# The last product's weights are multiplied with the gate on GpSimd before their split, and what its banks held is added to the sum first

## The chip, the cores and the metric

The kernel runs on one core of one Trainium2 chip. The metric is the device time of one execution in microseconds, the median of several runs. The engines of the core are TensorE (PE, with its weight loads PEld), VectorE (DVE), ScalarE (ACT), GpSimd (POOL) and SyncE (SP), which issues most transfers.

## The reference, cut to what matters

One layer (`DEPTH = 1`) on 512 tokens of width 2048, and a last RMSNorm:

```python
mod = cond @ w_ada[l] + b_ada[l]
shift, scale, gate = jnp.split(mod, 3, axis=-1)
h = rms_norm(x, norm_g[l]) * (1.0 + scale[:, None, :]) + shift[:, None, :]
z = h @ w_in[l]
...
y = jnp.concatenate([y_a, y_b], axis=-1) @ w_out[l]
x = x + gate[:, None, :] * y
...
return rms_norm(x, final_g)
```

y_a comes from a spatial gating unit, y_b from an attention with forget gates. The change lies in the last three lines only: the product with w_out, the gate, the sum with x and the final norm. The gate is one number for each column of the output, so it can be multiplied with the columns of w_out ahead of the product as well as with the result behind it.

## The kernel before, in words

All matrix products are made in three passes. An operand is split in a high and a low half of float32r by `split` (L65): ScalarE copies to `hi`, VectorE (or GpSimd) takes `lo = src - hi`. A product is then hi·hi + lo·hi + hi·lo; `mm_part` (L1056) issues these three matmuls of 128x512 into one PSUM bank.

The stages before the last compute h, the projections, the gating unit and the attention; the gate's columns are summed on GpSimd in the middle of the kernel (`gate_step`, L714). The result y lies transposed in sixteen blocks of 128 rows and 512 tokens.

**The output projection.** It has 512 tokens and 2048 output columns, and is made in two units, `unit(0)` and `unit(1)` (L1110), of 1024 columns each: group g1 and group g2 of 512 columns. Inside a unit it is a fast 2x2 block product with seven block products in place of eight, in Winograd's form. The blocks are the two halves of the tokens (tiles t = 0, 1 and 2, 3 of 128 tokens), the two halves of y and the two column groups. Sums of w_out's blocks were made earlier and lie in DRAM (`tsum`). The order in a unit is A11, S3, S2, S1, A22, A12, S4. Each of them is eight k-blocks times two token tiles, 48 matmuls, into two banks (V, Z or X).

**Weights.** A product goes through four steps (`product`, L1062). For each step a weight tile `raw` of 128x1024 is loaded on SP (`wget` L1026 from w_out, or `w_sum` L1117 from `tsum`), split by `wsplit` (L1033: low half on VectorE, L67), and multiplied. The tag `raw` has four buffers, and the x tile of `base` (L1075) takes one of the four. The weights are named after their products: p5 for S1, p4 for A22, p2 for A12, p3 for S4.

**The last unit.** In `unit(1)` group g2 = 3 of the token tiles 0 and 1 is finished last. Its sum has the parts u2 (from S2 and A11), S1 and S4:

- `base` (L1075) makes u2·gate + x ahead of A12;
- S1 lies in the two banks Z; `u3 = Z + u3` (L1155) has read it for the other token tiles, and S4 accumulates on top of it in the same banks (`mm_part(..., False, ...)`, L1206);
- `total` (L1208) multiplies the bank Z = S1 + S4 with the gate into `tmp` (helper `gated`, L1072) and adds u2 (L1211);
- `norm` (L1213) squares the sum on ScalarE (L1092), adds the mean square to that of the other groups (L1216) and takes the power -1/2 on GpSimd (L1217); `put` (L1222) scales the rows and stores them.

S4's weights are loaded after A12's in the program and split in halves of 512 columns on their own (`w3h`, `w3l`, L1181 to L1188), with a priority that moves loads and splits forward. Ahead of the last product in the program stand the pieces of the other groups: `piece` (L1094) is a sum with x (L1087), a square (L1092) and a multiplication with final_g (L1098); `scale_out` (L1100) takes a power on GpSimd, then scales and stores the token tiles 2 and 3.

**What sets the order.** A scheduler orders each engine's instructions ahead of the run: the ready instruction that comes first in the program, where loads and splits of weights count as 150 instructions earlier (`high_priority(offset=WPRI)`), as do the reads of finished banks (`evac`, EPRI). Buffers of a tag are given out in this order when one comes free. On the chip each engine then follows its list strictly. `issue_after` fixes an order on one engine.

The functions that the diff touches:

Of the kernel before, what the change touches and what calls it, by code (L numbers as in the profile page):

```python
# [9 lines left out]
F32R = mybir.dt.float32r  # L10
BF16 = mybir.dt.bfloat16
AF = mybir.ActivationFunctionType
ALU = mybir.AluOpType
AX = mybir.AxisListType

P = 128
S = 512
# [10 lines left out]
def trunk_kernel(  # L28
# [17 lines left out]
    nc = tc.nc  # L46
# [12 lines left out]
    def bank(tag, name):  # L59
        if tag == "x":  # L60
            tag = "bbbc"[turn[0] % 4]
            turn[0] += 1
        return ps.tile([P, 512], F32, tag=tag, name=name, bufs={"mm": 4, "b": 3, "c": 1}[tag])

    def split(hi, lo, src, eng=None):  # L65
        a = nc.scalar.activation(hi, src, AF.Copy)  # L66
        return a, (eng or nc.vector).tensor_tensor(lo, src, hi.bitcast(F32), ALU.subtract)  # L67
# [34 lines left out]
    newest_mm = [None]  # L102
# [15 lines left out]
    WPRI = 150  # L118
# [4 lines left out]
    def w_tile(segs, k0, nk, src=win_r, name="", pri=WPRI, loeng=None, after=None):  # L123
        n = sum(w for _, w in segs)
        es = ExitStack()
        for p in list(pins):
            p[0] -= 1
            if p[0] < 0:
                es.enter_context(tc.issue_after(p[1].ins))
                pins.remove(p)  # L130
        with es, tc.high_priority(offset=pri):
            raw = wp.tile([P, nk, n], F32, tag="raw", name=f"raw_{name}", bufs=4)
            o = 0
            for c0, w in segs:
                newest_w[0] = (load if pri == 0 else nc.sync.dma_start)(
                    raw[:, :, o : o + w], src[:, k0 : k0 + nk, c0 : c0 + w]
                )
                o += w
            hi = wp.tile([P, nk, n], F32R, tag="whi", name=f"whi_{name}")
            lo = wp.tile([P, nk, n], F32R, tag="wlo", name=f"wlo_{name}")  # L140
            nc.scalar.activation(hi, raw, AF.Copy)  # L141
            with ExitStack() as es:
                if after is not None:
                    es.enter_context(tc.issue_after(after.ins))
                (loeng or nc.vector).tensor_tensor(lo, raw, hi.bitcast(F32), ALU.subtract)  # L145
        return hi, lo

    def tick():
        if slots:
            for f in slots.pop(0):  # L150
                f()
        if fillers:
            fillers.pop(0)()
# [88 lines left out]
    gate = gp_.tile([P, 4, 512], F32, name="gate")  # L242
# [211 lines left out]
    for q, (k0, nk) in enumerate(CH):  # L454
# [10 lines left out]
        for si, sid in enumerate(order):  # L465
# [12 lines left out]
            for kk, n_k, gi in steps:  # L478
                    segs, bl = grp[gi]
                    hi, lo = w_tile(  # L480
                        segs, kk, n_k, name=f"st{q}_{sid}_{gi}_{kk}", pri=0,
                        loeng=nc.gpsimd if gi in POOLG and q + kk + si > 0 else None,
                        after=first_h[0] if q + kk + si == 0 else None,
                    )
# [31 lines left out]
    pb = ctx.enter_context(tc.tile_pool(name="pb", bufs=1))  # L516
# [506 lines left out]
    def wtile(name):  # L1023
        return wp.tile([P, 2, 512], F32, tag="raw", name=name, bufs=4)

    def wget(dst, half, g, i):  # L1026
        k = 8 * half + 2 * i
        nc.sync.dma_start(dst, wout_r[:, k : k + 2, g * 512 : (g + 1) * 512])
        return dst
# [3 lines left out]
    def wsplit(src, name):  # L1033
        nsplit[0] += 1
        if nsplit[0] % 3 == 0:
            hi = pb.tile([P, 2, 512], F32R, tag="pth", name=f"whi_{name}")
            lo = pb.tile([P, 2, 512], F32R, tag="ptl", name=f"wlo_{name}")
        else:
            hi = wp.tile([P, 2, 512], F32R, tag="whi", name=f"whi_{name}")
            lo = wp.tile([P, 2, 512], F32R, tag="wlo", name=f"wlo_{name}")  # L1040
        newest_hl[:] = split(hi, lo, src)
        return hi, lo

    def lhs(kind, i, tt):
        if kind == "S4":
            c = slice(tt * P, (tt + 1) * P)
            return s4[i][:, 0, c], s4[i][:, 1, c]
        h_, l_, k, off = {
            "A11": (yh, yl, 8 + i, 0), "S3": (yh, yl, 8 + i, H),
            "A12": (yh, yl, i, 0), "A22": (yh, yl, i, H),  # L1050
            "S1": (sh_, sl_, i, 0), "S2": (sh_, sl_, i, H),
        }[kind]
        c = slice(off + tt * P, off + (tt + 1) * P)
        return h_[k][:, c], l_[k][:, c]

    def mm_part(bank_, kind, i, tt, hi, lo, begin, end):  # L1056
        h_, l_ = lhs(kind, i, tt)
        nc.tensor.matmul(bank_, h_, hi, start=begin, stop=False, skip_group_check=True)
        nc.tensor.matmul(bank_, l_, hi, start=False, stop=False, skip_group_check=True)  # L1059
        newest_mm[0] = nc.tensor.matmul(bank_, h_, lo, start=False, stop=end, skip_group_check=True)  # L1060

    def product(banks, kind, weights, begin, steps=range(4)):  # L1062
        for i2 in steps:
            with tc.high_priority(offset=WPRI):
                hi, lo = weights(i2)
            for j in range(2):
                for tt in range(2):
                    i = 2 * i2 + j
                    mm_part(banks[tt], kind, i, tt, hi[:, j, :], lo[:, j, :], begin and i == 0, i == 7)
            tick()  # L1070

    def gated(rr, src, g):  # L1072
        nc.vector.tensor_tensor(rr, src, gate[:, g, :], ALU.mult)

    def base(rr, g):  # L1075

        xr = wtile("xr3")
        for t in range(2):
            nc.sync.dma_start(xr[:, t, :], x[0, t * P : (t + 1) * P, g * 512 : (g + 1) * 512])
        for t in range(2):  # L1080
            gated(rr[t], rr[t], g)
            nc.vector.tensor_tensor(rr[t], rr[t], xr[:, t, :], ALU.add)
# [27 lines left out]
    def unit(u):  # L1110
        g1, g2 = 2 * u, 2 * u + 1
        V = [bank("mm", f"woV{u}_{t}") for t in range(2)]

        def w_raw(half, g, name):
            return lambda i: wsplit(wget(wtile(f"{name}_{u}_{i}"), half, g, i), f"{name}_{u}_{i}")
# [8 lines left out]
        def tiles(n, tag, b=2):  # L1124
            pool = act if tag == "yb" else pb
            return [pool.tile([P, S], F32, name=f"{n}{u}_{t}", tag=tag, bufs=b) for t in range(2)]

        def evac(f):
            with tc.high_priority(offset=EPRI):
                for t in range(2):  # L1130
                    f(t)
# [8 lines left out]
        Z = [bank("mm" if u else "x", f"woZ{u}_{t}") for t in range(2)]  # L1140
# [5 lines left out]
        if u:  # L1146
            wide = [pb.tile([P, 2, 512], F32, name=f"wide{t}", tag="wsp", bufs=2) for t in range(2)]
            u2, u3 = [w[:, 0, :] for w in wide], [w[:, 1, :] for w in wide]
        else:
            u2, u3 = tiles("u2", "yb", 8), tiles("u3", "yb", 8)  # L1150
# [16 lines left out]
        both(lambda t: gated(c7[t], c7[t], g1))  # L1167
        both(lambda t: piece(c7[t], 2 + t, g1))
        if u:
            base(u2, g2)  # L1170
        product(V, "A12", w_raw(0, g1, "p2"), False)
        evac(lambda t: gated(c1[t], V[t], g1))
        both(lambda t: piece(c1[t], t, g1))
        if u == 0:
# [2 lines left out]
            both(lambda t: gated(u2[t], u2[t], g2))  # L1177
            both(lambda t: piece(u2[t], t, g2))
            return
        w3 = []  # L1180
        for i in range(4):  # L1181
            with tc.high_priority(offset=WPRI):
                a = wget(wtile(f"p3_{u}_{i}"), 0, g2, i)
                for j in range(2):
                    hi = pb.tile([P, S], F32R, tag="qstk", bufs=8, name=f"w3h{2 * i + j}")
                    lo = pb.tile([P, S], F32R, tag="kstk", bufs=8, name=f"w3l{2 * i + j}")
                    split(hi, lo, a[:, j, :])
                    w3.append((hi, lo))  # L1188
        before = newest_mm[0]
        for t in range(2):  # L1190
            tk = 2 + t
# [9 lines left out]
        def mm(t):  # L1201
            for i in range(8):
                with ExitStack() as es:
                    if i == 0:
                        es.enter_context(tc.issue_after(before.ins))
                    mm_part(Z[t], "S4", i, t, w3[i][0], w3[i][1], False, i == 7)  # L1206

        def total(t):  # L1208
            tmp = pb.tile([P, S], F32, name=f"tmp{t}", tag="sgB", bufs=4)
            gated(tmp, Z[t], g2)  # L1210
            return tmp, nc.vector.tensor_tensor(u2[t], tmp, u2[t], ALU.add)  # L1211

        def norm(t, tmp):  # L1213
            s0, s1 = sfin[:, t, 0:1], sfin[:, t, 1:2]
# [7 lines left out]
        def put(t, g, eng, q):  # L1222
# [6 lines left out]
            q.dma_start(out[0, t * P : (t + 1) * P, g * 512 : (g + 1) * 512], rr)  # L1229

        mm(0)
        norm(0, total(0)[0])
        put(0, 0, nc.scalar, nc.sync)
        put(0, 1, nc.scalar, nc.sync)
        mm(1)
        tmp, last = total(1)
        with tc.issue_after(last.ins):
            put(0, 2, nc.vector, nc.sync)
# [8 lines left out]
    for u in range(2):  # L1247
        unit(u)
# [26 lines left out]
```

## Time and profile before

| | us |
|---|---|
| runs, median of 3 | 898.06 (897.68 to 898.46) |
| the profiled execution | 899.12 |
| its span in the profile | 897.4 |
| granted TensorE clock | 0.997 |
| PE, DVE, ACT, POOL busy | 881.7, 614.7, 444.4, 479.7 |
| HBM read, written | 166.90 MB, 20.97 MB |

Lines such as `L1073` are lines of the kernel; helpers show their own line. A row of the timeline is start, duration, engine, line, operation, out<-in by tile name, shape, and in brackets how long the engine had been idle and what ended that. Buffer numbers are left out of tile names: `p` are the weight tiles p2 to p7 and p3, `wide` are u2 and u3 of unit 1, `c` are c1 and c7. Durations of neighbouring instructions on one engine overlap by some 0.08 us; the distance of their starts is what one costs in a full queue. In a table by stretches each engine has its busy time and, in brackets, its number of instructions; then come granted clock, DMA share and GB/s.

### The profile page before, as it was taken

How to read it: one execution, taken by the hardware profiler on the slowest of the kernel's cores; microseconds unless marked ns; L12 is line 12 of the kernel's file. 1: busy time of each engine (PE TensorE's matmuls, PEld its weight loads, DVE VectorE, ACT ScalarE, POOL GpSimd, SP SyncE). 2: the span in 40 equal slices, each digit the busy share in tenths (PEclk: the TensorE clock that was granted, in tenths of full speed). 3: DMA queues.
4: the chain of work that ended last, by engine and by line, in shares of the span. 5: the costliest groups of instructions: out<-in, count | busy, mean ns of one | idle time of the engine just before them, and what ended most of it. 6: DMA issues, size and time to landing. Idle time of an engine off the chain costs nothing.

```text
span 897.4 us, 12688 instructions
## 1 busy us (share of the span) xinstructions
PE 881.7 (98%) x4453; PEld 744.7 (83%) x4453; DVE 614.7 (68%) x999; ACT 444.4 (50%) x778; POOL 479.7 (53%) x407
## 2 busy tenths in 40 slices
PE   9999999999999999999999999999999999999995
PEld 6788888887888897887889888998898888888884
DVE  5878888374427967563876664547664779997686
ACT  6653333452224224564656554556466567654454
POOL 1266554515676269999799779957566520000001
PEclk9999999999999999999999999999999999999998
DMA  9999996348986275544443536466666466577575
GB/s 340 354 352 355 354 344 205 111 134 284 331 285 200 61 212 155 156 139 136 142 150 117 187 107 188 129 193 198 222 188 211 165 214 200 174 263 244 178 245 195
DMA packets 123216, 188.91 MB, mean 211 GB/s; under 512 B 9856, under 2 KB 86864, under 8 KB 122640
## 3 DMA queue, kind: packets, MB, share of 16 engines
q1 hardware_dynamic: 113248, 153.97, 53.6%
q0 software_dynamic: 9472, 33.56, 11.6%
q8 instruction: 35, 0.57, 0.3%
q10 hardware_dynamic: 432, 0.57, 0.2%
q14 instruction: 29, 0.24, 0.1%
HBM read 166.90 MB, written 20.97 MB: 209 GB/s over the span
## 4 chain that ended last, share of the span: by engine, by line
PE 89%; DMA 4%; DVE 3%; ACT 1%; issue 1%; SPq 1%; POOLq 0%; POOL 0%; ACTq 0%
PE s L163 6%; PE s L165 6%; PE s L164 6%; PE k L165 3%; PE gb L164 3%; PE gb L165 3%; PE gb L163 3%; PE k L164 3%; PE k L163 3%; PE vb L173 3%; PE vb L174 3%; PE va L175 3%; PE va L174 3%; PE va L173 3%; PE vb L175 3%; PE q L165 3%
## 5 line engine op out<-in xcount | busy, mean ns | idle before, releaser
L723 POOL TENSOR_SCALAR gate<-gate,sc 128x512 f32<-128x512 f32 x64 | 108.5, 1708 | 1.4
L727 POOL TENSOR_TENSOR gate<-gate,gate 128x512 f32<-128x512 f32 x60 | 91.1, 1518 | 2.4
L145 POOL TENSOR_TENSOR wlo_st<-raw_st,whi_st 128x768 fp32r<-128x768 f32 (+3 forms) x33 | 66.0, 2001 | 45.0 <-ACT whi_st L141 39.8
L163 PE MATMUL s<-hh,whi_st 128*128 128x512 f32 x224 | 86.2, 391 | 0.9 <-ACT sp L501 0.9
L164 PE MATMUL s<-hl,whi_st 128*128 128x512 f32 x224 | 86.2, 389 | 0.0
L66 ACT ACTIVATE whi_p<-p 128x1024 fp32r<-128x1024 f32 x52 | 55.2, 1061 | 57.2 <-PE woZ L1059 22.1
L1102 POOL TENSOR_TENSOR sfin<-sfin,nhalf 128x1 f32<-128x1 f32 x2 | 1.5, 746 | 149.6 <-DVE sfin L1194 149.6
L285 DVE SCALAR_TENSOR_TENSOR acc<-ada,sc,acc 128x512 f32<-128x512 f32 x98 | 73.9, 754 | 6.2 <-DMA ada<-in_w_ada_dram 3.4
L67 DVE TENSOR_TENSOR wlo_p<-p,whi_p 128x1024 fp32r<-128x1024 f32 x52 | 63.4, 1221 | 19.6 <-ACT whi_p L66 19.5
L165 PE MATMUL s<-hh,wlo_st 128*128 128x512 f32 x224 | 75.3, 391 | 0.0
L173 PE MATMUL vb<-whi_vb,hh 128*128 128x256 f32 (+1 forms) x256 | 72.3, 285 | 0.8 <-DVE sgA L442 0.5
L174 PE MATMUL vb<-whi_vb,hl 128*128 128x256 f32 (+1 forms) x256 | 72.3, 285 | 0.0
L175 PE MATMUL vb<-wlo_vb,hh 128*128 128x256 f32 (+1 forms) x256 | 70.7, 284 | 0.0
L141 ACT ACTIVATE whi_st<-raw_st 128x768 fp32r<-128x768 f32 (+3 forms) x35 | 31.1, 890 | 68.6 <-PE s L164 49.3
L775 POOL TENSOR_TENSOR ts<-ts 128x256 f32<-128x256 f32 x64 | 57.0, 903 | 13.2 <-DMA ts<-in_w_out_dram 11.4
L67 DVE TENSOR_TENSOR ptl<-p,pth 128x512 fp32r<-128x512 f32 (+1 forms) x64 | 45.4, 733 | 14.1 <-ACT pth L66 13.0
L145 DVE TENSOR_TENSOR wlo_va<-raw_va,whi_va 128x1024 fp32r<-128x1024 f32 x16 | 24.6, 1538 | 39.3 <-ACT whi_va L141 39.3
L163 PEld LDWEIGHTS s<-hh,whi_st 128*128 128x128 f32 x224 | 42.0, 188 | 10.2 <-ACT sp L501 1.7
L163 PE MATMUL k<-hh,whi_k 128*128 128x512 f32 x128 | 50.4, 394 | 0.0
L163 PE MATMUL q<-hh,whi_q 128*128 128x512 f32 x128 | 50.4, 394 | 0.0
L164 PE MATMUL q<-hl,whi_q 128*128 128x512 f32 x128 | 50.4, 394 | 0.0
L173 PE MATMUL va<-whi_va,hh 128*128 128x512 f32 x128 | 50.3, 393 | 0.0
(317 smaller groups left out, 2628.0 us busy)
## 6 DMA issues: line engine op xcount, KB each, us to landing
ada<-in_w_ada_dram SPq DMA_DIRECT2D x128, 256.0 KB
gate<-in_w_ada_dram POOLq DMA_DIRECT2D x32, 512.0 KB, 4.4
p<-ts SPq DMA_DIRECT2D x32, 512.0 KB
p<-in_w_out_dram SPq DMA_DIRECT2D x24, 512.0 KB
raw_st<-in_w_in_dram SPq DMA_DIRECT2D x22, 384.0 KB
raw_va<-in_w_in_dram SPq DMA_DIRECT2D x16, 512.0 KB
raw_q<-in_w_in_dram SPq DMA_DIRECT2D x16, 512.0 KB
raw_k<-in_w_in_dram SPq DMA_DIRECT2D x16, 512.0 KB
```

Of the source, the lines that this page charges most:

```text
L67: return a, (eng or nc.vector).tensor_tensor(lo, src, hi.bitcast(F32), ALU.subtract)
L145: (loeng or nc.vector).tensor_tensor(lo, raw, hi.bitcast(F32), ALU.subtract)
L163: nc.tensor.matmul(pt, hi[:, j, cs], hh[k], start=(k == first), stop=False)
L164: nc.tensor.matmul(pt, hi[:, j, cs], hl[k], start=False, stop=False)
L165: newest = nc.tensor.matmul(pt, lo[:, j, cs], hh[k], start=False, stop=(k == last))
L173: nc.tensor.matmul(o, ah[k][:, tsl], hi[:, j, :], start=(k == first), stop=False)
L174: nc.tensor.matmul(o, al[k][:, tsl], hi[:, j, :], start=False, stop=False)
L175: nc.tensor.matmul(o, ah[k][:, tsl], lo[:, j, :], start=False, stop=(k == last))
L285: nc.vector.scalar_tensor_tensor((sb if kk == KB - 1 else a)[:, :, c_], ga[:, j, :, c_], col, a[:, :, c_], ALU.mult, ALU.add,)
L723: nc.gpsimd.tensor_scalar(ga[:, j] if kk else a, ga[:, j], sc[:, kk : kk + 1], None, ALU.mult)
L727: done = nc.gpsimd.tensor_tensor(a, a, ga[:, j], ALU.add)
L775: done = nc.gpsimd.tensor_tensor(dst, l, r, ALU.subtract)
```

## The change

`base` gets the banks Z and adds what they hold (S1) to u2 first, then multiplies with the gate and adds x. The banks of S4 are new ones (`woY`), so that S4 starts from nothing. Each of S4's four weight tiles is multiplied with the gate's columns on GpSimd, in two halves, between its load and its split; its load and splits stand between the steps of A12 in the program now and no longer behind them. The end then only adds: `u2 = Z + u2`.

```diff
-    def base(rr, g):
+    def base(rr, g, Z):
 
         xr = wtile("xr3")
         for t in range(2):
             nc.sync.dma_start(xr[:, t, :], x[0, t * P : (t + 1) * P, g * 512 : (g + 1) * 512])
+        for t in range(2):
+            nc.vector.tensor_tensor(rr[t], Z[t], rr[t], ALU.add)
         for t in range(2):
             gated(rr[t], rr[t], g)
             nc.vector.tensor_tensor(rr[t], rr[t], xr[:, t, :], ALU.add)
...
         if u:
-            base(u2, g2)
-        product(V, "A12", w_raw(0, g1, "p2"), False)
+            base(u2, g2, Z)
+            Z = [bank("x", f"woY{t}") for t in range(2)]
+        w3 = []
+
+        def w_last(i):
+            with tc.high_priority(offset=WPRI):
+                a = wget(wtile(f"p3_{u}_{i}"), 0, g2, i)
+                for j in range(2):
+                    nc.gpsimd.tensor_tensor(a[:, j, :], a[:, j, :], gate[:, g2, :], ALU.mult)
+                    hi = pb.tile([P, S], F32R, tag="qstk", bufs=8, name=f"w3h{2 * i + j}")
+                    lo = pb.tile([P, S], F32R, tag="kstk", bufs=8, name=f"w3l{2 * i + j}")
+                    split(hi, lo, a[:, j, :])
+                    w3.append((hi, lo))
+
+        for i in range(4):
+            product(V, "A12", w_raw(0, g1, "p2"), False, (i,))
+            if u and i:
+                w_last(i - 1)
+        if u:
+            w_last(3)
         evac(lambda t: gated(c1[t], V[t], g1))
...
-        w3 = []
-        for i in range(4):
-            with tc.high_priority(offset=WPRI):
-                a = wget(wtile(f"p3_{u}_{i}"), 0, g2, i)
-                for j in range(2):
-                    hi = pb.tile([P, S], F32R, tag="qstk", bufs=8, name=f"w3h{2 * i + j}")
-                    lo = pb.tile([P, S], F32R, tag="kstk", bufs=8, name=f"w3l{2 * i + j}")
-                    split(hi, lo, a[:, j, :])
-                    w3.append((hi, lo))
...
                     if i == 0:
-                        es.enter_context(tc.issue_after(before.ins))
-                    mm_part(Z[t], "S4", i, t, w3[i][0], w3[i][1], False, i == 7)
+                        es.enter_context(tc.issue_after((newest_mm[0] if t else before).ins))
+                    mm_part(Z[t], "S4", i, t, w3[i][0], w3[i][1], i == 0, i == 7)
 
         def total(t):
             tmp = pb.tile([P, S], F32, name=f"tmp{t}", tag="sgB", bufs=4)
-            gated(tmp, Z[t], g2)
-            return tmp, nc.vector.tensor_tensor(u2[t], tmp, u2[t], ALU.add)
+            return tmp, nc.vector.tensor_tensor(u2[t], Z[t], u2[t], ALU.add)
```

## Prediction

> **What bounds the kernel now.** I read the page first (busy time, slices, chain of waits), then the last 50 us, where the change lies: busy time by stretch, the vector engine's waits, and the timeline of each engine.
>
> ```profile
> PE 881.7 (98%) x4453; PEld 744.7 (83%) x4453; DVE 614.7 (68%) x999; ACT 444.4 (50%) x778; POOL 479.7 (53%) x407
> POOL 1266554515676269999799779957566520000001
> PE 89%; DMA 4%; DVE 3%; ACT 1%; issue 1%; SPq 1%; POOLq 0%; POOL 0%; ACTq 0%
> ```
>
> TensorE is busy for 98% of the span and carries 89% of the chain; GpSimd (POOL) is empty over the last slices. DVE's 68% is a mean, so it has to be read by stretch:
>
> ```profile
> 855.00:860.00 5.00, 5.00 (x24) 4.14 (x23) 4.11 (x6) 2.12 (x2) 0.00 (x0) 1.00 0.67 205
> 860.00:865.00 5.00, 5.00 (x24) 4.14 (x23) 5.00 (x8) 3.35 (x6) 0.00 (x0) 1.00 0.67 219
> 865.00:870.00 5.00, 5.00 (x24) 4.14 (x23) 5.00 (x8) 1.06 (x1) 0.00 (x0) 1.00 0.96 315
> 870.00:875.00 5.00, 5.00 (x24) 4.14 (x23) 4.50 (x8) 4.49 (x10) 0.00 (x0) 1.00 0.69 229
> 875.00:880.00 5.00, 5.00 (x24) 4.14 (x23) 4.61 (x11) 2.08 (x4) 0.81 (x1) 1.00 0.09 32
> 880.00:885.00 5.00, 5.00 (x24) 4.14 (x23) 5.00 (x14) 3.90 (x8) 0.68 (x2) 1.00 0.64 236
> ```
>
> After length and PE come PEld, DVE, ACT and POOL. PE never stops, so the end of its stream cannot come earlier; but DVE is full as well, with 5.00 of 5 us in three of these six stretches. All the time for which DVE stood idle from 856 to 888, and PE's last instruction, are these rows:
>
> ```profile
> DVE wide L1082 <- DMA xr<-in_x_dram: 1.3, 1, 1.3
> DVE w3l L67 <- ACT w3h L66: 0.9, 2, 0.5
> DVE tmp L1073 <- PE woZ L1060: 0.4, 1, 0.4
> ...
> 887.40 0.39 PE L1060 MATMUL woZ<-w3l,s 128*128 128x512 f32 x1
> ```
>
> The first idle time ends as the stretch begins. Behind it DVE has 0.9 us of slack in its queue and 0.4 us just ahead of the last sum: 1.3 us in 32. That margin is what the change spends.
>
> **What the change removes.** The last product's sum is the end of the kernel:
>
> ```profile
> 884.99 0.68 DVE L1073 TENSOR_TENSOR tmp<-woZ,gate 128x512 f32<-128x512 f32 x1
> ...
> 887.24 0.16 DVE L1216 SCALAR_TENSOR_TENSOR sfin<-ssf,sfin 128x1 f32<-128x1 f32 x1
> 887.83 0.69 DVE L1073 TENSOR_TENSOR tmp<-woZ,gate 128x512 f32<-128x512 f32 x1 [0.43 <-PE woZ L1060]
> 888.56 0.69 DVE L1211 TENSOR_TENSOR wide<-tmp,wide 128x512 f32<-128x512 f32 x1
> ...
> 890.56 0.15 DVE L1216 SCALAR_TENSOR_TENSOR sfin<-ssf,sfin 128x1 f32<-128x1 f32 x1
> 891.37 0.48 DVE L1228 TENSOR_SCALAR fin<-fin,sfin 128x512 f32<-128x512 f32 x1 [0.66 <-POOL sfin L1217]
> ```
>
> After the last matmul the old kernel multiplies the bank with the gate (887.83) and only then adds it to u2 (888.56). The multiplication goes: 888.56 - 887.83 = 0.73 us off the path, for each of the two tiles, and the second lies on the end. The square, L1216, the power on GpSimd, the scaling and the stores follow as before, up to the span's end at 897.4. So 9.57 us from 887.83 become 8.84. That is the whole gain, since PE's stream stays.
>
> **What it adds on DVE.** `base` now starts with two sums of the S1 bank, and the two multiplications behind them can no longer run before S1 is done:
>
> ```profile
> 847.91 0.68 DVE L1073 TENSOR_TENSOR wide<-wide,gate 128x512 f32<-128x512 f32 x1
> ...
> 849.12 0.69 DVE L1073 TENSOR_TENSOR wide<-wide,gate 128x512 f32<-128x512 f32 x1
> ...
> 855.89 0.69 DVE L1082 TENSOR_TENSOR wide<-wide,xr 128x512 f32<-128x512 f32 x1 [1.33 <-DMA xr<-in_x_dram]
> 856.50 0.68 DVE L1155 TENSOR_TENSOR wide<-woZ,wide 128x512 f32<-128x512 f32 x1
> 857.10 0.68 DVE L1082 TENSOR_TENSOR wide<-wide,xr 128x512 f32<-128x512 f32 x1
> ```
>
> One instruction takes a slot of 0.60 us (856.50 to 857.10). The two multiplications ran at 847.91 and 849.12, ahead of the full stretch, and move into it: 1.2 us. The two new sums have the form of L1155 and come on top: 1.2 us. The two L1082 sums stay in the stretch, only later. Taken out ahead of the last sum is one multiplication of 0.6 (that of 884.99). Net 1.8 us. DVE was through with tile 0 at 887.40 (887.24 + 0.16), so it reaches the last sum between 888.3 (the 0.9 of idle time filled) and 889.2 (not filled), where the last matmul is done at 887.8. That delays the sum by 0.5 to 1.4 us against 887.83; less the 0.73 saved, -0.2 to +0.7, and I take +0.2. So the moved work alone eats the gain, and all the queue's margin with it.
>
> **What it adds on GpSimd.** Eight multiplications of 128x512, two for each of the four weight tiles, between the load and the split. The nearest row is the gate's own sum, the same shape with two SBUF inputs; beside it one DVE split of the same size:
>
> ```profile
> L727 POOL TENSOR_TENSOR gate<-gate,gate x60: 1274/1292/2912, 329.0 to 580.7; 128x512 f32<-128x512 f32 x60
> L67 DVE TENSOR_TENSOR w3l<-p,w3h x8: 679/682/693, 871.2 to 879.0; 128x512 fp32r<-128x512 f32 x8
> ```
>
> 8 x 1.29 = 10.3 us on an idle engine would be free if the two engines did not meet. They do:
>
> ```profile
> 208.00 1.73 POOL L753 TENSOR_TENSOR tspth<-tspth 128x512 f32<-128x512 f32 x1
> 209.69 2.26 POOL L753 TENSOR_TENSOR ts<-ts 128x512 f32<-128x512 f32 x1
> ...
> 208.85 1.96 DVE L145 TENSOR_TENSOR wlo_va<-raw_va,whi_va 128x1024 fp32r<-128x1024 f32 x1 [0.26 <-ACT whi_va L141]
> ...
> L145 DVE TENSOR_TENSOR wlo_va<-raw_va,whi_va x16: 1215/1270/2223, 187.2 to 269.6; 128x1024 fp32r<-128x1024 f32 x16
> L67 DVE TENSOR_TENSOR wlo_p<-p,whi_p x52: 1212/1219/1227, 729.6 to 873.0; 128x1024 fp32r<-128x1024 f32 x52
> ```
>
> The same split takes 1.21 to 1.23 us in all 52 cases while GpSimd is quiet, and up to 2.22 where it works. At 208.85 it took 1.96: GpSimd's instruction ended at 209.73, and 209.73 + 1.22 = 210.95 is, within 0.15, where the split ended (210.81). Then it was GpSimd's turn to wait: the one issued at 209.69 took 2.26 and not 1.29. So such instructions run one after the other, not side by side. The Trainium skill, page "SBUF — State Buffer", section "Who interferes with whom", says this as a rule against such a change: a VectorE instruction with two SBUF inputs shares a read interface with GpSimd's reads, and the second to issue is blocked until the first is through. The trace agrees (the 0.74 us of wait at 208.85); by the rule in full, all 10.3 us are added, and the time would be 898.06 + 0.2 + 10.3 = 908.6, which lies inside the forecast's own range below and has its chance there.
>
> In the full stretch most of DVE's work has two SBUF inputs (splits, sums with x, multiplications with the gate or with final_g); only those that read a bank (woX, woV, woZ) go free. The price of one multiplication lies between nothing (it falls on idle time or on an instruction that reads a bank) and 1.29. The row at 208.85 shows 0.74 where DVE came late to a GpSimd instruction that had run for 0.85 us; with a full DVE queue the next instruction stands ready at once and waits for nearly all of it. I take 0.85: 8 x 0.85 = 6.8 us. If instead DVE's queue keeps GpSimd out, w3's splits come late, and DVE and ScalarE wait in their order for them: about the same loss by another way.
>
> **What is queued behind the new waits.** On ScalarE each w3 high half now waits for GpSimd, with the last A12 split and the squares behind it. On GpSimd the two powers of `scale_out` stand behind the multiplications, and eight of the stores behind those. On DVE all of c1's pieces and the scaling stand ahead of the last sum, because they precede it in the program. On SP the loads now go p2_0, p2_1, p3_0, p2_2, p3_1, p2_3:
>
> ```profile
> 862.48 0.37 SPq L1028 DMA_DIRECT2D p<-in_w_out_dram  x1
> ...
> 864.28 6.21 DMA p<-in_w_out_dram
> ...
> 872.99 1.22 DVE L67 TENSOR_TENSOR wlo_p<-p,whi_p 128x1024 fp32r<-128x1024 f32 x1
> ...
> 874.03 0.39 PE L1058 MATMUL woV<-whi_p,yh 128*128 128x512 f32 x1
> ```
>
> p2_3 was asked for at 862.48; its low half ended at 874.21, and PE begins its step at 874.03. Two loads ahead of it, a load that takes up to 6.21 us, and a fourth buffer that the x tiles hold until `base` is done can bring it 1 to 3 us late.
>
> **Sum.** -0.73 + 0.93 (together +0.2) + 6.8 = +7.0 us. The profiled execution took 899.12 us, a span of 897.4 and 1.7 around it: 904.4 and 906.1. It is 1.06 above the median of 898.06; on the median the sum gives 905.1. This case's own range goes from 8 x 0.5 with -0.2 (901.9) to 10.3 with +0.7 (909.1).
>
> **Rivals.** (1) Not slower: the multiplications fall where DVE reads banks or waits, so that DVE still reaches the last sum before PE is done. Then 0.73 us go and the time is 897.3. It decides as long as less than 1.3 us is added to DVE's queue ahead of the last sum; the count of 1.8 speaks against it, GpSimd's empty row for it. (2) DVE's moved work alone, without a price for the shared reads: 898.3. Speaking for it: instructions that read banks did not wait, and some of the eight can fall there. (3) The load order stops PE for 1 to 3 us at A12's last step, with the reads hardly meeting: 898.3 + 1 to 3 = 899.3 to 901.3, say 900.3. For it speaks that p2_3 has next to no slack. That the change does not do what it says is hardly possible: the multiplication of the bank is gone from `total`.
>
> **How the numbers follow.** Forecast 0.62; rival (1) 0.13; rival (2) 0.13; rival (3) 0.12. A measurement of this kernel tells about 0.2% (1.8 us) from no change, so faster means under 896.3 and slower over 899.9. Slower: the forecast and half of (3), 0.68. Same: most of (1), (2) and the rest of (3), 0.28. Faster would need 1.8 us from a tail that gives 0.73: 0.04. The range of 8 in 10 goes from 897.6, between (1) and (2), to the forecast's upper end 909.1; it leaves out (1) and a little above.
>
> **What would show it.** Right: GpSimd shows eight multiplications of 1.3 us or more between about 862 and 884; DVE's splits and sums there show 1.5 to 2.5 us where they had 0.68 and 1.22; the last sum comes at 893 to 897 and its wait names DVE, not PE, or PE's stream shows waits on w3. Wrong: DVE rows in that stretch keep 0.68 and 1.22, or the last sum starts within 1 us of 887.8; a PE stall at A12's last step alone would be rival (3).

## The result, and the profile after

The changed kernel takes 907.52 us (906.26 to 909.33, 5 runs) where the kernel before takes 898.07 (897.68 to 898.57) beside it: a ratio of 1.010, interval 1.0087 to 1.0113, or 9.45 us more (7.8 to 10.1). The profiled execution took 909.33 us, its span is 907.6; against the span before (897.4) that is 10.2 us. 1.47 of these are there before the last product stage, where nothing was changed: 2.6 arise in the first 50 us, where the granted clock happened to be 0.93 instead of 1.00, and 1.1 go again between 420 and 580. The rest arises in the last 40 us. In the changed kernel's line numbers the bodies of the last stages stand two lines lower (L1087 is L1089, L1098 is L1100); the multiplication on GpSimd is L1180, the last sum L1221.

The page of the changed kernel, busy time, slices of GpSimd and shares of the chain:

```profile
PE 887.7 (98%) x4453; PEld 748.2 (82%) x4453; DVE 624.3 (69%) x999; ACT 445.6 (49%) x778; POOL 493.1 (54%) x415
POOL 1255654515676279999898789867565510000051
PE 86%; DVE 5%; DMA 4%; issue 2%; ACT 1%; SPq 1%; POOL 0%; POOLq 0%; DVEq 0%; ACTq 0%
```

Apart from shifts of a tenth or two, one slice of GpSimd has changed (the last but one, 0 to 5), and PE is still busy for 98%. The means hide all of it again. The table by stretches of the changed kernel (PE, PEld, DVE, ACT, POOL with their numbers of instructions, then granted clock, DMA share, GB/s) doesn't:

```profile
865.00:870.00 5.00, 5.00 (x24) 4.14 (x23) 5.00 (x7) 1.31 (x3) 0.16 (x1) 1.00 0.82 250
870.00:875.00 5.00, 4.28 (x18) 3.05 (x18) 3.40 (x5) 2.10 (x3) 3.13 (x3) 1.00 0.76 258
875.00:880.00 5.00, 3.02 (x12) 1.81 (x11) 5.00 (x4) 2.93 (x5) 4.01 (x4) 1.00 0.45 147
880.00:885.00 5.00, 1.82 (x4) 1.49 (x5) 5.00 (x5) 2.39 (x5) 4.29 (x3) 0.69 0.20 66
885.00:890.00 5.00, 5.00 (x16) 3.92 (x15) 5.00 (x11) 2.05 (x4) 2.08 (x3) 0.63 0.00 0
```

Two columns differ from the table of before that the prediction shows. DVE is 5.00 of 5 us busy from 875 to 885 with 9 instructions, where it had done 25 (11 and 14): its rows are fewer and longer. And PE, which never stopped, falls to 3.02 and 1.82; from 885 to 890 it is busy throughout, but makes 16 matmuls in 5 us instead of 24, at a granted clock of 0.63.

What the waits of the changed kernel say, from 855 us on (engine, what waited, who released it: us in total, times, longest):

```profile
ACT w3h L66 <- POOL p L1180: 9.0, 4, 4.8
PEld woV L1060 <- DVE wlo_p L67: 6.1, 2, 4.9
PE woV L1060 <- DVE wlo_p L67: 5.2, 2, 4.5
...
DVE wide L1221 <- PE woY L1060: 2.3, 1, 2.3
...
PE woV L1058 <- ACT whi_p L66: 0.6, 1, 0.6
```

PE waits for the low halves of A12's weights (`wlo_p`), above all for that of its last step. The last sum (L1221) waits for PE, 2.3 us: DVE is there in time. The timelines of the changed kernel show how it comes about, GpSimd first:

```profile
869.84 2.53 POOL L1180 TENSOR_TENSOR p<-p,gate 128x512 f32<-128x512 f32 x2 [138.21 <-DVE c L1168]
874.24 3.26 POOL L1180 TENSOR_TENSOR p<-p,gate 128x512 f32<-128x512 f32 x2 [1.87 <-DMA p<-in_w_out_dram]
878.49 2.95 POOL L1180 TENSOR_TENSOR p<-p,gate 128x512 f32<-128x512 f32 x2 [0.99 <-DVE w3l L67]
882.15 3.80 POOL L1180 TENSOR_TENSOR p<-p,gate 128x512 f32<-128x512 f32 x2 [0.71 <-DMA p<-in_w_out_dram]
```

```profile
874.59 1.77 DVE L1073 TENSOR_TENSOR c<-c,gate 128x512 f32<-128x512 f32 x1
876.28 1.77 DVE L67 TENSOR_TENSOR w3l<-p,w3h 128x512 fp32r<-128x512 f32 x1
877.97 0.68 DVE L1089 TENSOR_TENSOR c<-c,xr 128x512 f32<-128x512 f32 x1
878.57 1.75 DVE L67 TENSOR_TENSOR w3l<-p,w3h 128x512 fp32r<-128x512 f32 x1
880.25 1.74 DVE L1089 TENSOR_TENSOR c<-c,xr 128x512 f32<-128x512 f32 x1
881.91 1.21 DVE L67 TENSOR_TENSOR wlo_p<-p,whi_p 128x1024 fp32r<-128x1024 f32 x1
883.05 1.77 DVE L67 TENSOR_TENSOR w3l<-p,w3h 128x512 fp32r<-128x512 f32 x1
884.74 1.76 DVE L1100 TENSOR_TENSOR c<-c,fgb 128x512 f32<-128x512 f32 x1
```

Read the two together. While GpSimd multiplies, a DVE instruction of 0.68 us takes 1.75 to 1.77; in the gaps (877.97, 881.91) the rows have their old 0.68 and 1.21. Six rows are longer by 1.06 to 1.09 each. The low half at 881.91 is the one that A12's last step needs. ScalarE had its high half done by 877.42:

```profile
876.38 1.04 ACT L66 ACTIVATE whi_p<-p 128x1024 fp32r<-128x1024 f32 x1
```

It came 4.5 us later, behind rows that had lost 1.09 (874.59), 1.09 (876.28), 1.07 (878.57) and 1.06 (880.25): 4.3 us. PE, in the changed kernel's timeline:

```profile
878.27 0.39 PE L1059 MATMUL woV<-whi_p,yl 128*128 128x512 f32 x1
883.18 1.22 PE L1060 MATMUL woV<-wlo_p,yh 128*128 128x512 f32 x2 [4.52 <-DVE wlo_p L67]
884.20 0.63 PE L1058 MATMUL woV<-whi_p,yh 128*128 128x512 f32 x1
884.63 0.63 PE L1059 MATMUL woV<-whi_p,yl 128*128 128x512 f32 x1
```

Matmuls stand 0.23 us apart in this kernel, so the step from 878.27 to 883.18 lost 4.68. Two smaller stops (0.89 at 874.72, 0.81 at 877.47) went before it. Ahead of the second, A12's high half stood on ScalarE behind a `w3h` that had waited 2.59 us for GpSimd's product (at 875.84), so a small part of the loss is that wait and not a longer row. After it the matmuls stand 0.43 apart until 888.8: 13 of them cost some 2.7 us more. With what is left in small gaps PE loses 9.39 us, and the last matmul starts at 898.34. From the last sum (898.77) to the span's end are 8.83 us, where 9.57 were from the multiplication before it: 0.74 saved. 1.47 + 9.39 - 0.74 = 10.1 of the 10.2 us.

### The profile page after: what moved, and what is told of

Same layout as the page of the kernel before. It is cut to its first block, busy times and chain, and to the rows that moved or that the text cites. A ratio compares the mean times of both kernels' runs of the same rounds, so it can differ in the third digit from the quotient of the medians.

```text
span 907.6 us, 12710 instructions
## 1 busy us (share of the span) xinstructions
PE 887.7 (98%) x4453; PEld 748.2 (82%) x4453; DVE 624.3 (69%) x999; ACT 445.6 (49%) x778; POOL 493.1 (54%) x415
## 4 chain that ended last, share of the span: by engine, by line
PE 86%; DVE 5%; DMA 4%; issue 2%; ACT 1%; SPq 1%; POOL 0%; POOLq 0%; DVEq 0%; ACTq 0%
PE s L164 6%; PE s L165 6%; PE s L163 5%; PE gb L164 3%; PE gb L165 3%; PE gb L163 3%; PE va L173 3%; PE va L174 3%; PE va L175 3%; PE vb L174 3%; PE vb L173 3%; PE vb L175 3%; PE k L165 3%; PE k L164 3%; PE k L163 3%; PE q L165 3%
## 5 line engine op out<-in xcount | busy, mean ns | idle before, releaser
L723 POOL TENSOR_SCALAR gate<-gate,sc 128x512 f32<-128x512 f32 x64 | 111.0, 1746 | 1.4
L1180 POOL TENSOR_TENSOR p<-p,gate 128x512 f32<-128x512 f32 x8 | 12.5, 1587 | 141.8 <-DVE c L1168 138.2
L164 PEld LDWEIGHTS s<-hl,whi_st 128*128 128x128 f32 x224 | 42.9, 192 | 10.0 <-POOL hl L314 0.9
```

The costliest lines, as they stand in the source:

```text
L164: nc.tensor.matmul(pt, hi[:, j, cs], hl[k], start=False, stop=False)
L723: nc.gpsimd.tensor_scalar(ga[:, j] if kk else a, ga[:, j], sc[:, kk : kk + 1], None, ALU.mult)
```

## The experiments

All ratios are to the kernel before, run beside the experiment on the same chip; they differ from the quotient of the two medians by up to 0.2%. PE's losses are sums over the gaps between starts of matmuls in the last 50 us of the profiled execution, as above.

**The moved work alone** (`e1_base_alone`). `base` and the new banks as changed, the multiplication at the end and the late weights as before:

```diff
-                    nc.gpsimd.tensor_tensor(a[:, j, :], a[:, j, :], gate[:, g2, :], ALU.mult)
...
-        for i in range(4):
-            product(V, "A12", w_raw(0, g1, "p2"), False, (i,))
-            if u and i:
-                w_last(i - 1)
-        if u:
-            w_last(3)
+        product(V, "A12", w_raw(0, g1, "p2"), False)
         evac(lambda t: gated(c1[t], V[t], g1))
+        if u:
+            for i in range(4):
+                w_last(i)
...
-            return tmp, nc.vector.tensor_tensor(u2[t], Z[t], u2[t], ALU.add)
+            gated(tmp, Z[t], g2)
+            return tmp, nc.vector.tensor_tensor(u2[t], tmp, u2[t], ALU.add)
```

> Base and the new banks alone: S1 is added in base first, S4 starts in banks of its own, nothing is multiplied on GpSimd, the end multiplies S4 with the gate as before, and S4's weights come after A12's as before. Port theory (GpSimd's multiplications and DVE's instructions with two SBUF inputs shut one another out, and this is nearly all of the loss): the moved work alone costs what the prediction counted without the saving, +0.2 + 0.73 = about +0.9, 899.0 us, PE without a wait. Order theory (the loss is that S4's weights stand between A12's): the same 899.0, since that order is gone. Moved-work theory (DVE's 1.8 us more in a full queue push the splits late and stop PE): 903 us or more with PE waiting for a low half.

Measured: 898.79 us against 898.81, ratio 0.999 (0.9978 to 1.0001), no gap in PE's stream. The moved work costs nothing. DVE in this run:

```profile
854.07 0.69 DVE L1157 TENSOR_TENSOR wide<-woZ,wide 128x512 f32<-128x512 f32 x1
854.68 0.68 DVE L1081 TENSOR_TENSOR wide<-woZ,wide 128x512 f32<-128x512 f32 x1
...
887.39 0.69 DVE L1073 TENSOR_TENSOR tmp<-woY,gate 128x512 f32<-128x512 f32 x1 [0.30 <-PE woY L1060]
```

The new sum (L1081) needs no x tile. It fills the 1.3 us in which DVE had waited for that tile before (the row at 855.89), and DVE still waits 0.30 us for PE at the end.

**The change without its eight multiplications** (`e2_no_mult`): the line L1180 is left out.

> The changed kernel without the eight multiplications (S4 goes without its gate); base, banks, program order as changed. Port theory: DVE's splits and sums keep 0.68 and 1.22 us, PE does not stop for longer than 0.5 us, and the time is 897.3 to 898.5. Order theory: the last A12 split still comes late behind S4's splits, PE stops for 2 to 5 us at A12's last step, 901 to 905.

Measured: 899.76 us, ratio 1.0002 (0.9986 to 1.0017). The median is 1.3 us above what was expected, and PE does stop for longer than 0.5 us; the ratio says no change. DVE's rows have their 0.68 and 1.23. PE loses 1.70 us, 1.15 of it at A12's last step, whose tile is loaded later; the wait of this run is

```profile
PE woV L1058 <- ACT whi_p L66: 1.0, 1, 1.0
```

That is the predicted rival (3), real and small. It eats the 0.73 of the tail.

**The load order** (`e4_late_order`): multiplications kept, but loads, multiplications and splits of S4's weights behind A12 as before (the second hunk of `e1_base_alone`).

> The changed kernel with S4's loads, multiplications and splits behind A12 in the program, as S4's weights stood before. Port theory: the eight multiplications still meet DVE's full queue, so DVE rows of 1.7 to 1.8 us stay and 5 to 8 us are lost, now at S4's weights and at the last sum in place of A12's last step: 902 to 906. Order theory: A12's last split is no longer held up and the loss goes: 897.3 to 899.

Measured: 907.0 us, ratio 1.0073 (1.0051 to 1.0094), about as the whole change and 1 us above what the theory of the shared reads had named. PE now waits in S4 (views: GpSimd's timeline, and the waits):

```profile
871.67 13.17 POOL L1180 TENSOR_TENSOR p<-p,gate 128x512 f32<-128x512 f32 x8 [142.76 <-DMA p<-in_w_out_dram]
```

```profile
PE woY L1060 <- DVE w3l L67: 4.0, 4, 2.4
```

The place of the stop moved with the order, the loss stayed (9.40 us of PE). So the order decides where PE stops, not how long.

**Waiting for GpSimd, without its reads** (`e6_memset`): each multiplication becomes three writes of a constant.

```diff
-                    nc.gpsimd.tensor_tensor(a[:, j, :], a[:, j, :], gate[:, g2, :], ALU.mult)
+                    nc.gpsimd.memset(a[:, j, :], 0.01)
+                    nc.gpsimd.memset(a[:, j, :], 0.01)
+                    nc.gpsimd.memset(a[:, j, :], 0.01)
```

> Each multiplication is replaced by three writes of a constant over the same half tile on GpSimd (S4 then has constant weights): S4's splits wait for GpSimd as long or longer, 1.6 us for each half by the memset rows against 1.29, but GpSimd reads nothing. Port theory: DVE's rows in that stretch keep 0.68 and 1.22 us, PE stops for at most 1 or 2 us, and the time is at most 901. Order theory (waiting for GpSimd's result is what holds up ScalarE's and DVE's queues): the loss stays or grows, 906 to 910.

Measured: 901.23 us (898.98 to 905.12), ratio 1.0019 (1.0002 to 1.0035). GpSimd and DVE in the profiled execution, which was the longest of these runs:

```profile
875.40 0.99 POOL L1180 MEMSET p<- 128x512 f32 x2 [3.08 <-DMA p<-in_w_out_dram]
876.33 1.00 POOL L1181 MEMSET p<- 128x512 f32 x2
877.27 1.00 POOL L1182 MEMSET p<- 128x512 f32 x2
```

```profile
876.03 0.68 DVE L67 TENSOR_TENSOR w3l<-p,w3h 128x512 fp32r<-128x512 f32 x1
876.63 0.69 DVE L1073 TENSOR_TENSOR c<-c,gate 128x512 f32<-128x512 f32 x1
```

A tile stays with GpSimd for 2.87 us (875.40 to 878.27), inside the 2.53 to 3.80 of the multiplications, so a split gets its tile about as late. DVE's rows beside the writes keep 0.68. The Trainium skill, page "SBUF — State Buffer", section "Who interferes with whom", says that a GpSimd instruction which only writes doesn't contend with VectorE's second input; these rows agree.

The time is 0.2 us over the 901 that was expected at most. The waits of this execution limit what the experiment says:

```profile
ACT whi_p L66 <- DMA p<-in_w_out_dram: 8.2, 2, 6.9
...
ACT w3h L66 <- POOL p L1182: 2.6, 3, 2.0
```

The longest of PE's stops here (1.39 us idle at 874.31, of 3.9 us lost in all) follows a tile of A12's weights that landed late: ScalarE had waited 6.9 us for that load, and not for GpSimd. For GpSimd it waited only 2.6 us in all, against 9.0 in the change, because in this schedule A12's high halves stand ahead of w3's. So waiting is tested here only in part. That it adds little is seen better in the next experiment, which takes it out.

**Its reads, without waiting** (`e5_side`): the product goes to a tile that nobody reads, and the splits take the raw weights.

```diff
+        if u:
+            scr = pb.tile([P, 4, 512], F32, name="scr", tag="vs")
...
-                    nc.gpsimd.tensor_tensor(a[:, j, :], a[:, j, :], gate[:, g2, :], ALU.mult)
+                    nc.gpsimd.tensor_tensor(scr[:, j, :], a[:, j, :], gate[:, g2, :], ALU.mult)
```

> GpSimd still makes the eight multiplications of the loaded weights, but into a tile that nobody reads; the splits take the raw weights at once (S4 goes without its gate). Nobody waits for GpSimd's result, only the load buffer's release does. Port theory: DVE rows of 1.7 to 1.8 us stay, and most of the loss: 902 to 907. Rival (waiting for the product): DVE rows fall back to 0.68 and 1.22, time as without multiplications, 898 to 900.

Measured: 907.16 us, ratio 1.0089 (1.0072 to 1.0106). GpSimd and DVE in this run:

```profile
878.10 7.18 POOL L1183 TENSOR_TENSOR scr<-p,gate 128x512 f32<-128x512 f32 x4 [0.68 <-DMA p<-in_w_out_dram]
```

```profile
880.17 2.28 DVE L67 TENSOR_TENSOR wlo_p<-p,whi_p 128x1024 fp32r<-128x1024 f32 x1
882.38 3.44 DVE L1089 TENSOR_TENSOR c<-c,xr 128x512 f32<-128x512 f32 x2
```

Now nothing waits for a product, and the loss is there in full: the split of 1.21 takes 2.28, the sums of 0.68 take 1.72 each. PE loses 8.66 us, 5.01 at A12's last step; with the waits it was 9.39. The time is 0.2 us over the expected range. `e5_side` and `e2_no_mult` compute the same and differ only in GpSimd's eight instructions: this pair shows that its reads are the cause. The four kernels stand as a table (ratio to the kernel before):

| | GpSimd reads | GpSimd doesn't read |
|---|---|---|
| the splits wait for GpSimd | 1.010 (the change) | 1.0019 (`e6_memset`, a shorter wait) |
| they don't wait | 1.0089 (`e5_side`) | 1.0002 (`e2_no_mult`) |

**Half of the multiplications** (`e8_half`): only those with `j == 0`.

> Only the first half of each weight tile is multiplied on GpSimd, four instructions in place of eight (the other half goes without its gate). Port theory: each blocked DVE row costs about 1.1 us, so about half of the loss stays if the price is per instruction: 902 to 904. If the loss hangs on a point (DVE late enough to stop PE, and then the halved clock on top), much less than half: 899.5 to 901.5.

Measured: 903.56 us, ratio 1.0054 (1.0038 to 1.007): as expected, about half of the loss. PE loses 4.73 us, its longest stop 2.24, and the granted clock stays at 1.00.

**PE kept busy in its wait** (`e9_keep_busy`): in A12's last step, ahead of the low half, PE makes 18 matmuls into a bank that nobody reads.

```diff
+                    for _ in range(18):
+                        with tc.issue_after(d.ins):
+                            d = nc.tensor.matmul(idle, yh[0][:, 0:P], yh[0], start=True, stop=True, skip_group_check=True)
```

> The changed kernel, with 18 matmuls that nobody reads put into PE's 4.7 us wait at A12's last step; DVE's and GpSimd's order is unchanged. If the half granted clock behind that wait (matmuls 0.43 us apart and not 0.23) comes from PE's idling, it goes, and 2.5 us are saved: 904 to 906 with the wait itself still there. If the clock has another cause, the time stays at 907 to 908.

Measured: 906.39 us, ratio 1.0087 (1.0072 to 1.0102): 0.4 us over the expected range, and the intervals of this and of the change overlap. PE in this run:

```profile
876.27 4.26 PE L1076 MATMUL idle<-yh 128*128 128x512 f32 x18
881.00 0.74 PE L1079 MATMUL woV<-wlo_p,yh 128*128 128x512 f32 x2 [0.47 <-DVE wlo_p L67]
881.58 0.39 PE L1058 MATMUL woV<-whi_p,yh 128*128 128x512 f32 x1
881.81 0.40 PE L1059 MATMUL woV<-whi_p,yl 128*128 128x512 f32 x1
...
889.06 0.50 PE L1060 MATMUL woY<-w3l,s 128*128 128x512 f32 x1 [0.73 <-DVE w3l L67]
```

The low half comes as late as ever, but the matmuls behind it stand 0.23 apart and not 0.43. So the half clock belongs to PE's standing idle. Of its 2.7 us only a part comes back: a faster S4 meets w3's low halves, which are still late (0.73 idle at 889.06), and the last matmul comes 1.45 us earlier than after the change, once what the two executions differ by ahead of the stage is taken off. From there to the span's end it takes 0.7 us longer than after the change (9.97 against 9.26), so that only about half of the 1.45 us is left in that execution; why the end is longer wasn't traced.

**The multiplications on DVE** (`e3_mult_dve`): `nc.vector` instead of `nc.gpsimd` in L1180.

> The eight multiplications run on DVE in place of GpSimd, all else as changed. Port theory: on DVE each costs its slot of 0.60 us, 4.8 us in all, less than the 1.08 us that each blocked DVE row lost to GpSimd, so the kernel is faster than with GpSimd: 901 to 904. If GpSimd's multiplications cost DVE nothing (rival: the loss is the wait for the product, or the order), adding 4.8 us to DVE's full queue makes it slower than the changed kernel: 909 or more.

Measured: 905.09 us, ratio 1.007 (1.0055 to 1.0085). It misses what was expected by 1 us, and is still no slower than the multiplications on GpSimd: 8 x 0.60 us of DVE's own time come to 4.8, where the blocked rows had come to 6.9. PE loses 5.2 us in this run, in stops of at most 2.2, and never falls to half pace, so part of what is saved against the change is the clock.

**The multiplications at another time** (`e7_early`, `e11_spread`, `e10_early_mean`). The product of weights and gate is made while the products begin, stored, and loaded at the end; the rest is as in `e4_late_order`.

```diff
+    def pre_gate(i):
...
+            nc.gpsimd.dma_start(a, wout_r[:, 2 * i : 2 * i + 2, 3 * 512 : 4 * 512])
+        for j in range(2):
+            done = nc.gpsimd.tensor_tensor(a[:, j, :], a[:, j, :], gate[:, 3, :], ALU.mult)
...
+    parts.extend([lambda i=i: pre_gate(i) for i in range(4)])
...
-                a = wget(wtile(f"p3_{u}_{i}"), 0, g2, i)
+                a = wtile(f"p3_{u}_{i}")
+                nc.sync.dma_start(a, tg[i].rearrange("p (j n) -> p j n", j=2))
```

> The same sums as the changed kernel, with the eight multiplications made earlier: GpSimd multiplies S4's weights behind the sums of w_out's blocks (after 700 us), stores them in DRAM, and the end loads them ready multiplied, behind A12's. Port theory: no GpSimd read meets DVE in the last 50 us; DVE's rows keep 0.68 and 1.22 us, PE does not stop, the end is 0.73 us shorter than before: 897.0 to 898.2, a ratio of 0.9985 to 1.0. If base's moved work alone costs more than it seems, or the multiplications hurt as much where they went: 900 or more.

Measured: 909.3 us (904.41 to 912.16), ratio 1.0108 (1.0083 to 1.0134). That is a clear miss, and the trace says why. GpSimd and PE of this run:

```profile
748.50 10.30 POOL L793 TENSOR_TENSOR pg<-pg,gate 128x512 f32<-128x512 f32 x4 [3.47 <-DMA pg<-in_w_out_dram]
```

```profile
770.12 0.50 PE L1074 MATMUL woX<-whi_p,sh 128*128 128x512 f32 x1 [1.69 <-ACT whi_p L66]
...
773.79 1.22 PE L1076 MATMUL woX<-wlo_p,sh 128*128 128x512 f32 x2 [2.48 <-DVE wlo_p L67]
774.82 0.63 PE L1074 MATMUL woX<-whi_p,sh 128*128 128x512 f32 x1
775.24 0.63 PE L1075 MATMUL woX<-whi_p,sl 128*128 128x512 f32 x1
```

The multiplications landed at 732 to 773, in the first product stage, where DVE is as full as in the last one; the four at 748.50 took 2.6 us each and not 1.29. PE stopped three times between 758 and 774 (6.6 us) and lost some 8.4 with the slower clock behind it; the last 50 us show no stop. The same collision, at another place. A variant that also takes the mean ahead of the last multiplication with final_g (`e10_early_mean`) has it too:

```diff
-            nc.vector.scalar_tensor_tensor(s1, ssf[:, t, g2 : g2 + 1], 1.0 / D, s0, ALU.mult, ALU.add)
+            mean = nc.vector.scalar_tensor_tensor(
+                s1, ssf[:, t, g2 : g2 + 1], 1.0 / D, s0, ALU.mult, ALU.add
+            )
...
+            with tc.issue_after(mean.ins):
+                nc.vector.tensor_tensor(fin, u2[t], fgs[g2], ALU.mult)
```

> As e7_early, and the mean square of the last tile (which stood behind the multiplication with final_g in DVE's queue, 890.56 for a square done at 890.07) is taken ahead of it. Port theory: another 0.4 to 0.5 us at the end: 896.5 to 897.7. If the stores' landing sets the end, nothing: as e7_early.

Measured: 906.81 us (902.13 to 908.1), ratio 1.0074 (1.0049 to 1.01). Its runs scatter too far, and overlap those of `e7_early` too much, to read anything for the mean's own place. The last try puts the four tiles beside earlier steps:

```diff
-    parts.extend([lambda i=i: pre_gate(i) for i in range(4)])
+    for i, k in enumerate((7, 9, 11, 13)):
+        parts[k] = lambda f=parts[k], i=i: (f(), pre_gate(i))
```

> As e7 (the product of S4's weights with the gate is made early on GpSimd, stored, and loaded at the end), but the four tiles' multiplications are put with single steps of the sums of the weights, at about 700 to 735 us, where DVE is busy for 50 to 70% of most stretches, instead of behind them all at 732 to 759, where it is full. Theory of the shared reads with a full DVE queue: what a multiplication blocks is slack here, PE keeps its pace, and only the tail's saving is left: 897.3 to 899.5, so 6 us or more below e7. Rival: eight multiplications cost GpSimd and DVE their 8 to 9 us wherever they stand, since GpSimd is itself half busy there and its later sums are pushed into the full stretch: 904 to 909, as e7. Between the two, 900 to 903: the pushed sums collide in part; PE's waits at 740 to 775 would show it.

Measured: 905.24 us (903.83 to 908.42), ratio 1.0073 (1.0051 to 1.0096). The theory's number is missed again. GpSimd and the waits of this run:

```profile
751.20 9.17 POOL L775 TENSOR_TENSOR ts<-ts 128x256 f32<-128x256 f32 x4
```

```profile
PEld woZ L1077 <- DVE wlo_p L67: 1.9, 1, 1.9
...
PEld woX L1077 <- DVE wlo_p L67: 1.5, 1, 1.5
```

The multiplications did come earlier, two at a time from 646, 667, 699 and 718. But GpSimd had no room for them: its own last sums, done by 729 before, were pushed to 733 to 760, where four of them took 9.17 us beside full splits, and PE lost 4.4 us there. Its tail, 9.86 us from the last sum, is also a microsecond longer than that of the change; 0.3 of it lies between the sum and the scaling, where ScalarE's square comes later; the rest wasn't traced. So this is the expected rival, in number (904 to 909) and in kind: the pushed sums collide. Nor was DVE as empty as expected: from 710 to 720 it was busy for 4.97 and 4.94 of 5 us in the kernel before. Whether these eight multiplications have any place in this kernel that costs nothing stays open; two were tried, and neither is one.

## Why the prediction was right, point by point

The predicted 905.1 us against 907.52 measured: the direction, the likeliest case and the main cost, the shared reads, were right. The path by which that cost reaches the end was another, a second cost was missing, and the size was 2.4 us short.

- **What bounds the kernel.** Right that the end is PE's and that DVE's margin is what gets spent. The margin was read too small: the 1.3 us at 855.89 were set aside as lying at the stretch's beginning, but the wait for the x tile goes away when a sum that needs no x comes first (`e1_base_alone`).
- **The tail, -0.73.** Measured 0.74.
- **The moved work, +0.93.** Wrong by its whole size: `e1_base_alone` shows no difference, and DVE still reached the last sum 0.30 us ahead of PE.
- **The shared reads, 8 x 0.85 = 6.8.** Right in kind: reads without waiting cost 0.9%, the same kernel without them nothing (1.0002), and half of the reads half of the loss. In DVE's rows six instructions grew by 1.06 to 1.09 and the split at 871.82 (1.11 instead of 0.68) by 0.4: 6.9 us in all. That this comes so near to 6.8 is partly luck: a blocked row cost 1.08 and not 0.85, and six were blocked in full and not eight. The assumption that a DVE row which reads a bank isn't blocked held: in `e5_side` the sum with woX at 871.66 took 0.68, in the middle of a multiplication. GpSimd was also held up (12.5 us for eight instructions, 1.59 each instead of 1.29), as the row at 208.85 had let expect.
- **Where that reaches the end.** The working let DVE come late to the last sum. It doesn't: DVE waits 2.30 us for PE there. A12's last split stood behind four lengthened rows, and PE stopped for 4.68 us. The prediction had named this step, with a price only in rival (3), and had named A12's split behind ScalarE's highs, whose wait is there (9.0 us for `w3h`); it had not put the two together with the blocked rows. ScalarE's wait by itself costs little, 9.39 against 8.66 us of PE in `e5_side`.
- **The missing term.** No step of the prediction asks what PE does after a long stop. The matmuls at half pace cost 2.7 us, and `e9_keep_busy` wins 1.45 of it back by the last matmul. Term by term: forecast -0.73 + 0.93 + 6.8 = 7.0; traced -0.74, no moved work, 6.4 of stops (4.68, 0.89, 0.81), 2.7 of slow clock and 0.3 in small gaps, 8.65. The medians differ by 9.45; the 0.8 beyond 8.65 can't be placed by single executions.
- **Rival (1)**, hidden: it allowed DVE's queue less than 1.3 us more, and 6.9 came. DVE did reach the last sum before PE was done, but only because PE had been stopped. **Rival (2)**, the moved work alone: `e1_base_alone`, no difference. **Rival (3)**, the load order alone: `e2_no_mult`, a stop of 1.15 us, within its 1 to 3, but no loss that the ratio shows, since the tail's saving stands against it.
- **The rule in full, 908.6.** Nearer to 907.52 than the forecast, but not by its own working: DVE's rows grew by 6.9 us and not by 10.3, and the clock made up the difference.
- **The signs named.** Eight multiplications of 1.3 us or more between 862 and 884: they ran from 869.8 to 886. DVE rows of 1.5 to 2.5: 1.74 to 1.77. The last sum at 893 to 897 with a wait that names DVE, or PE waits on w3: it came at 898.77 and waited for PE, and PE's waits were on A12's weights.

## What to carry to other kernels

An engine that the profile shows empty isn't free when its reads and those of a full engine hold one another up, as GpSimd's and DVE's did here: before moving an elementwise step there, read the full engine's busy time by stretch, and count its instructions with two SBUF inputs in the very microseconds in which the step would run. Here doing the step on the full engine itself (4.8 us of its time) cost no more than doing it on the idle one (1.007 against 1.010). And a long stop of PE can have a second price behind it, in the clock: 2.7 us behind the stop of 4.68 here, nothing behind the stops of 2.24 and 1.75 in `e8_half`.

## What was not expected of the hardware

- After PE's stop of 4.5 us the granted clock was 0.69 and 0.63 in the next two stretches, and matmuls stood 0.43 us apart instead of 0.23 for 5.6 us. The Trainium skill, page "TensorE: Matmul & The Clock Gate", section "Part 1: The HAM clock gate", describes a halved clock after an idle window of about 3.4 us, and starts 426.7 ns apart at 512 columns. The spacing agrees. The length of the stop doesn't decide alone: in `e7_early` the same half pace followed two stops of 1.69 and 2.48 us with four matmuls between them, while `e8_half`, which lost 2.24 us at 874.5 and 1.75 at 879.1 with twelve matmuls between, kept its clock at 1.00.
- With both queues full, GpSimd and DVE took turns: a DVE instruction of 0.68 us took 1.77, a GpSimd one of 1.29 took 1.28 to 2.11. A DVE instruction that found GpSimd between two of its own ran in 0.68.
- Writes by GpSimd into the tiles that DVE reads next left DVE's rows unchanged (0.68 and 0.69 beside memsets).
